# A grouped convolution whose stores bound it: whole images in 16 KB rows, and a second pipeline that lags by half a group

## The chip, the cores and the metric

One core of one Trainium2 chip. The metric is the device time of one execution in microseconds (us); a kernel is run several times and the median is quoted. The engines are called as in the profile: PE (TensorE's matmuls), PEld (its weight loads), DVE (VectorE), ACT (ScalarE), POOL (GpSimd), SP (SyncE). The 16 DMA engines are called transfer engines; where the text speaks of the ends, packets or chains of an engine, one of these is meant.

## The reference

A 3x3 convolution with padding 1 in 8 groups: 16 images of 64 channels and 64x64 points, 128 output channels, all fp32.

```python
batch, c_in, h, w, c_out, k, groups = 16, 64, 64, 64, 128, 3, 8
for g in range(groups):            # 8 input and 16 output channels per group
    for b in range(batch):
        for co in range(c_out_per_group):
            for ci in range(c_in_per_group):
                for kh in range(k):
                    for kw in range(k):
                        output[b, g*16 + co] += weight[g*16 + co, ci, kh, kw] * x_pad[b, g*8 + ci, kh:kh+h, kw:kw+w]
```

It reads 16.8 MB and writes 33.6 MB.

## The kernel before

Two pipelines share TensorE. Each handles two images at a time: a "group" is those two images, in four "sets" of 16 image rows, each set in four PSUM banks (512 points each). A set is nine taps, one per "slot", and three empty slots for the eviction: a period of 12 slots. The pipelines use different tiles of the array and are 6 slots apart.

```python
xn = [pool.tile([128, H, W], BF16, name=f"xn{i}") for i in range(4)]     # all inputs, cast to bf16 by the loads
xs = [pool.tile([128, H, W], BF16, name=f"xs{i}") for i in range(4)]
ob = [pool.tile([128, HALF], FP32, name=f"ob{i}") for i in range(NOB)]   # NOB = 16 half images
...
def finish(self, st):                    # evict a set; store after every second set
    i, s = st // 4, st % 4
    if s % 2 == 0:
        self.slots = [(nob[0] + im) % NOB for im in range(2)]
        ...
    for j in range(2):
        for im in range(2):
            ...
            eng, copy = ((ACT, nc.scalar.copy), (DVE, nc.vector.tensor_copy))[nev[0] % 2]
            eng.wait((stored[slot], 16 * uses[slot]) if uses[slot] else None, self.full[j, im])
            free[b] = eng.done(copy(ob[slot][:, o0 : o0 + 512], banks[b]))
    ...
    if s % 2 == 1:
        s0 = HALF * (s // 2)
        for im in range(2):
            ...
            nc.sync.dma_start(outf[img][:, s0 : s0 + HALF], ob[slot]).then_inc(stored[slot], 16)

pipes = (Pipe(0), Pipe(1))
PERIOD, LAG, NSETS = T + 3, (T + 3) // 2, 16          # 12, 6, 16
for slot in range(PERIOD * NSETS + LAG):
    ...                                               # the matmuls of the live pipelines, tile by tile
```

In a slot the weights of one tap are loaded once per tile and used for two matmuls:

```python
if j == 0:
    PE.wait(w_need[wt.name, 3 * kh + kw])
    pe.ldweights(w_ap, **pos)
```

Of the kernel before, what the change touches and what calls it, by code (L numbers as in the profile page):

```python
# [7 lines left out]
FP32 = mybir.dt.float32  # L8
# [4 lines left out]
@with_exitstack  # L13
def kernel(
    ctx: ExitStack,
    tc: tile.TileContext,
    x: bass.AP,
    weight: bass.AP,
    groups: int,
    out: bass.AP,  # L20
):
    nc = tc.nc

    B, C, H, W = x.shape
    CO, CIg, K, _ = weight.shape
    G = groups
    COg = CO // G
    HW = H * W
    T = K * K
    assert (B, C, CO, K, G, H, W) == (16, 64, 128, 3, 8, 64, 64)  # L30

    R = 8
    NCH = H // R
    HALF = HW // 2

    HALF = HW // 2
    NOB = 16

    pool = ctx.enter_context(tc.tile_pool(name="sb", bufs=1))
    psum = ctx.enter_context(tc.tile_pool(name="psum", bufs=1, space=bass.MemoryType.PSUM))  # L40

    xn = [pool.tile([128, H, W], BF16, name=f"xn{i}") for i in range(4)]
    xs = [pool.tile([128, H, W], BF16, name=f"xs{i}") for i in range(4)]
    ob = [pool.tile([128, HALF], FP32, name=f"ob{i}") for i in range(NOB)]
    w_sb = pool.tile([128, CIg * T], FP32, name="w_sb")
    mask = pool.tile([128, G], FP32, name="mask")
    ident = pool.tile([128, 128], BF16, name="ident")
    E = pool.tile([128, T, 160], BF16, name="E")
    wN = pool.tile([128, T, 128], BF16, name="wN")
    wS = pool.tile([128, T, 128], BF16, name="wS")  # L50
    banks = [psum.tile([128, 512], FP32, name=f"bank{i}") for i in range(8)]

    with tc.tile_critical():  # L53
        program(nc, x, weight, out, xn, xs, ob, w_sb, mask, ident, E, wN, wS, banks)
# [29 lines left out]
def program(nc, x, weight, out, xn, xs, ob, w_sb, mask, ident, E, wN, wS, banks):  # L84
    H = W = 64
    HW, HALF, T, G, CIg, COg, R = H * W, H * W // 2, 9, 8, 8, 16, 8
    NOB = len(ob)
    sems = []
# [6 lines left out]
    def sem(name):  # L95
        s = nc.alloc_semaphore(name)
        sems.append(s)
        return s
# [80 lines left out]
    outf = out.rearrange("b co h w -> b co (h w)")  # L179
    taps = [(1, 1)] + [(a, b) for a in range(3) for b in range(3) if (a, b) != (1, 1)]  # L180
    pe = nc.tensor
    stored = [sem(f"st{i}") for i in range(NOB)]
    uses = [0] * NOB
    nob = [0]
    nev = [0]

    class Pipe:
# [52 lines left out]

        def finish(self, st):
            i, s = st // 4, st % 4
            if s % 2 == 0:
                self.slots = [(nob[0] + im) % NOB for im in range(2)]
                self.wrote = [[], []]
                nob[0] += 2
            for j in range(2):
                for im in range(2):
                    slot, b = self.slots[im], self.banks[j][im]
                    o0 = 512 * (2 * (s % 2) + j)  # L250
                    eng, copy = ((ACT, nc.scalar.copy), (DVE, nc.vector.tensor_copy))[nev[0] % 2]
                    nev[0] += 1
                    eng.wait((stored[slot], 16 * uses[slot]) if uses[slot] else None, self.full[j, im])
                    free[b] = eng.done(copy(ob[slot][:, o0 : o0 + 512], banks[b]))  # L254
                    self.wrote[im].append(free[b])
                nev[0] += 1
            nev[0] += 1
            if s % 2 == 1:
                s0 = HALF * (s // 2)
                for im in range(2):  # L260
                    slot = self.slots[im]
                    img = 2 * i + 8 * self.k + im
                    SP.wait(*self.wrote[im])
                    nc.sync.dma_start(outf[img][:, s0 : s0 + HALF], ob[slot]).then_inc(stored[slot], 16)
                    uses[slot] += 1

    pipes = (Pipe(0), Pipe(1))
    PERIOD, LAG, NSETS = T + 3, (T + 3) // 2, 16
    for slot in range(PERIOD * NSETS + LAG):
        live = []  # L270
        for p, lag in zip(pipes, (0, LAG)):
# [10 lines left out]

    SP.wait(*((stored[s], 16 * uses[s]) for s in range(NOB)))
    POOL.wait(SP.done(nc.sync.nop()))
# [36 lines left out]
```

## Time and profile before

| | before |
|---|---|
| median time | 130.17 us (3 runs), 130.13 us (6 runs) |
| span of the profiled execution | 128.2 us |
| PE busy | 86.9 us, 68%; idle from 93.5 us on, the last eviction ends at 94.7 |
| stores / loads, share of the 16 transfer engines | 62.9% / 32.8% |
| store transfers | 32 of 1 MB, rows of 8 KB |

The profile is read by stretches: until 20 us loads alone, until 55 us loads and stores mixed, then stores alone, for the last 32 us with all compute engines idle. The columns of the list of DMA queues are packets, MB and share of the 16 transfer engines' time, as in this line:

```profile
q8 instruction: 13, 0.21, 0.6%
```

Thirteen packets of 16 KB each: TensorE's instructions, fetched while it runs (with about 1000 of them taken out, below, there are nine).

### The profile page before, as it was taken

The numbers are of one execution on the slowest core, as the hardware profiler recorded it, in microseconds if no ns is written. First come the engines' busy times: TensorE is split into PE (matmuls) and PEld (weight loads), VectorE is DVE, ScalarE is ACT, GpSimd is POOL, SyncE is SP. The second block draws the span as 40 slices with busy tenths as digits, with TensorE's granted clock in tenths as the row PEclk, the third lists the DMA queues.
The fourth block names the chain that finished last, engine by engine and source line by source line (L and its number), as shares of the span: only waits on it lengthen the run. The fifth ranks groups of instructions, "written<-read, shape, count | busy, mean of one in ns | idle before, by whom it ended". The sixth has DMA issues, their size and how long they took to land.

```text
span 128.2 us, 3808 instructions
## 1 busy us (share of the span) xinstructions
PE 86.9 (68%) x2322; PEld 41.2 (32%) x1170; DVE 45.8 (36%) x74; ACT 37.0 (29%) x68; POOL 7.2 (6%) x19
## 2 busy tenths in 40 slices
PE   0199999999999999999999999999910000000000
PEld 0153353544435355444553544544500000000000
DVE  1840465446444645446544564465440000000000
ACT  4030354345333543336333453354330000000000
POOL 5960000000000000000000000000000000000000
PEclk9999999999999999999999999999996555555555
DMA  2999999999999999999999999999999999999950
GB/s 24 162 202 215 224 212 220 215 289 284 281 289 281 284 271 297 297 401 424 419 424 424 396 435 406 435 414 429 417 424 429 424 432 422 429 427 432 427 243 10
DMA packets 6271, 42.21 MB, mean 329 GB/s; under 512 B 848, under 2 KB 848, under 8 KB 1424
## 3 DMA queue, kind: packets, MB, share of 16 engines
q1 hardware_dynamic: 4752, 33.59, 62.9%
q0 software_dynamic: 1504, 8.39, 32.8%
q8 instruction: 13, 0.21, 0.6%
q14 instruction: 2, 0.02, 0.0%
HBM read 16.81 MB, written 33.55 MB: 393 GB/s over the span
## 4 chain that ended last, share of the span: by engine, by line
PE 67%; DVE 4%; issue 2%; POOL 1%; POOLq 0%; DVEq 0%; SPq 0%
PE bank L227 65%; DVE E L149 2%; DVE ob L254 2%; PE bank L162 2%; POOL ident L128 0%; POOL mask L123 0%; POOL mask L133 0%; POOL xn L106 0%; POOLq L123 0%; POOLq L316 0%; DVEq L75 0%; SPq L53 0%
## 5 line engine op out<-in xcount | busy, mean ns | idle before, releaser
L227 PE MATMUL bank<-xs,wS 32*64 32x504 bf16 (+3 forms) x1152 | 71.6, 374 | 0.6 <-issue 0.4
L227 PE MATMUL bank<-xn,wN 32*64 32x504 bf16 (+3 forms) x1152 | 71.8, 380 | 0.2 <-DVE ob L254 0.2
L254 DVE COPY ob<-bank 128x512 f32<-128x512 f32 x64 | 41.3, 686 | 45.4 <-PE bank L227 45.4
L254 ACT COPY ob<-bank 128x512 f32<-128x512 f32 x64 | 34.5, 589 | 51.2 <-PE bank L227 51.1
L222 PEld LDWEIGHTS <-wS 32*64 32x64 bf16 x576 | 27.5, 104 | 20.8 <-issue 9.9
L222 PEld LDWEIGHTS <-wN 32*64 32x64 bf16 x576 | 19.1, 106 | 25.0 <-issue 20.9
L162 PE MATMUL bank<-ident,E 128*128 128x128 bf16 x18 | 2.1, 313 | 5.9 <-DVE E L149 5.9
L106 POOL DMA_DIRECT2D xs<-in_x_dram x7 | 3.8, 543 | 0.0
L162 PEld LDWEIGHTS bank<-ident,E 128*128 128x128 bf16 x18 | 1.8, 148 | 5.9 <-DVE E L149 5.9
L149 DVE TENSOR_TENSOR E<-w_sb,mask 128x288 bf16<-128x288 f32 x5 | 2.9, 642 | 1.7 <-DMA w_sb<-in_weight_dram 1.7
L106 POOL DMA_DIRECT2D xn<-in_x_dram x5 | 2.9, 583 | 1.0 <-SPq L53 1.0
L172 ACT CAST wS<-bank 128x512 bf16<-128x512 f32 (+1 forms) x3 | 1.2, 487 | 5.2 <-PE bank L162 5.2
L172 DVE CAST wN<-bank 128x512 bf16<-128x512 f32 (+1 forms) x3 | 1.5, 551 | 0.7 <-PE bank L162 0.7
L172 ACT ACT_TABLE_LOAD x1 | 1.3, 1283 | 1.0 <-SPq L53 1.0
L117 DVE MEMSET mask<- 128x8 f32 x1 | 0.1, 65 | 1.1 <-SPq L53 1.1
L128 POOL TENSOR_SCALAR_AFFINE_SELECT ident<-ident 128x128 bf16<-128x128 bf16 x1 | 0.3, 306 | 0.0
L123 POOL TENSOR_SCALAR_AFFINE_SELECT mask<-mask 128x8 f32<-128x8 f32 x1 | 0.2, 211 | 0.1
L133 POOL TENSOR_SCALAR_AFFINE_SELECT mask<-mask 128x8 f32<-128x8 f32 x1 | 0.2, 199 | 0.0
L302 POOL MEMSET const-float32-0.0<- 128x1 f32 x1 | 0.1, 99 | 0.3 <-issue 0.3
L118 DVE MEMSET ident<- 128x64 uint32 x1 | 0.1, 112 | 0.0
L302 POOL MEMSET const-bfloat16-1.0<- 128x1 bf16 x1 | 0.1, 102 | 0.0
L302 POOL MEMSET const-uint8-127<- 128x1 uint8 x1 | 0.1, 102 | 0.0
(1 smaller groups left out, 0.1 us busy)
## 6 DMA issues: line engine op xcount, KB each, us to landing
out_dram<-ob SPq DMA_DIRECT2D x32, 1024.0 KB, 28.0
xn<-in_x_dram POOLq DMA_DIRECT2D x3, 1024.0 KB, 29.6
xs<-in_x_dram POOLq DMA_DIRECT2D x2, 1024.0 KB, 29.6
xn<-in_x_dram POOLq DMA_DIRECT2D x2, 512.0 KB, 7.6
xs<-in_x_dram POOLq DMA_DIRECT2D x2, 512.0 KB, 9.4
xs<-in_x_dram POOLq DMA_DIRECT2D x1, 768.0 KB, 48.4
xs<-in_x_dram POOLq DMA_DIRECT2D x2, 128.0 KB, 9.5
w_sb<-in_weight_dram SPq DMA_DIRECT2D x1, 36.0 KB, 1.8
```

The costliest lines, as they stand in the source:

```text
L106: nc.gpsimd.dma_start(t.rearrange("p h w -> p (h w)")[p0:p1, h0 * W : h1 * W], xr[row0 + p0 : row0 + p1, h0 * W : h1 * W],).then_inc(s, 16)
L117: m1 = DVE.done(nc.vector.memset(mask, 1.0))
L123: m3 = POOL.done(nc.gpsimd.affine_select(out=mask, in_=mask, compare_op=ALU.is_ge, fill=0.0, base=0, channel_multiplier=1, pattern=[[-COg, ...
L128: m4 = POOL.done(nc.gpsimd.affine_select(out=ident, in_=ident, compare_op=ALU.not_equal, fill=1.0, base=0, channel_multiplier=1, pattern=[ ...
L133: m5 = POOL.done(nc.gpsimd.affine_select(out=mask, in_=mask, compare_op=ALU.is_ge, fill=0.0, base=COg - 1, channel_multiplier=-1, pattern= ...
L149: e = DVE.done(nc.vector.tensor_mul(E[:, :, 32 * r : 32 * r + 32].rearrange("p t (g c) -> p t g c", c=CIg), wv.unsqueeze(2).to_broadcast([ ...
L162: ins = nc.tensor.matmul(banks[b][:, 128 * t : 128 * t + 128], E[:, t0 + t, off : off + 128], ident, start=True, stop=True,)
L172: free[b] = eng.done(copy(dst, banks[b][:, 0 : 128 * n]))
L222: pe.ldweights(w_ap, **pos)
L227: ins = pe.add_instruction(mybir.InstMatmult(name=nc.get_next_instruction_name(), engine=mybir.EngineType.PE, start_tensor_calc=k == 0, st ...
L254: free[b] = eng.done(copy(ob[slot][:, o0 : o0 + 512], banks[b]))
L302: nc = _bacc.Bacc("TRN2", target_bir_lowering=False, num_devices=1)
```

## The change

The intent: longer store rows, so half as many packets; an image is stored when it is complete. Whole images need buffers of twice the size, so there are eight for sixteen. With eight, both pipelines in step would hold all four pairs at once; the second one is therefore moved back by half a group (24 slots), so that pairs come free one at a time.

```diff
-    NOB = 16
+    NOB = 8
-    ob = [pool.tile([128, HALF], FP32, name=f"ob{i}") for i in range(NOB)]
+    ob = [pool.tile([128, HW], FP32, name=f"ob{i}") for i in range(NOB)]
 ...
-            if s % 2 == 0:
+            if s == 0:
                 self.slots = [(nob[0] + im) % NOB for im in range(2)]
 ...
-                    o0 = 512 * (2 * (s % 2) + j)
+                    o0 = 512 * (2 * s + j)
 ...
-            if s % 2 == 1:
-                s0 = HALF * (s // 2)
+            if s == 3:
                 for im in range(2):
 ...
-                    nc.sync.dma_start(outf[img][:, s0 : s0 + HALF], ob[slot]).then_inc(stored[slot], 16)
+                    nc.sync.dma_start(outf[img], ob[slot]).then_inc(stored[slot], 16)
 ...
-    PERIOD, LAG, NSETS = T + 3, (T + 3) // 2, 16
+    PERIOD, LAG, NSETS = T + 3, (T + 3) // 2 + 2 * (T + 3), 16
```

More of the change, by code (lines that the diff above doesn't have):

```diff
@@ L34 @@
     HALF = HW // 2
-    HALF = HW // 2
-    NOB = 16
+    NOB = 8
     pool = ctx.enter_context(tc.tile_pool(name="sb", bufs=1))
```

## The prediction

> **What bounds the kernel now.** I read the two rows of slices first, because they show which resource is full and when. Of the page of the kernel before:
>
> ```profile
> PE   0199999999999999999999999999910000000000
> PEclk9999999999999999999999999999996555555555
> DMA  2999999999999999999999999999999999999950
> GB/s 24 162 202 215 224 212 220 215 289 284 281 289 281 284 271 297 297 401 424 419 424 424 396 435 406 435 414 429 417 424 429 424 432 422 429 427 432 427 243 10
> ```
>
> A slice is 128.2 / 40 = 3.2 us. TensorE works from slice 2 to slice 29 and then does nothing for ten slices, a quarter of the span. The DMA engines are at 9 in every slice from 1 to 37. So TensorE isn't the bound, although the chain of waits gives it 67% of the span; that chain follows instructions and stops at the last eviction, near 94.7 us. The remaining 33 us are stores that were issued and have still to land.
>
> The second view is the DMA queues, which give the work in the engines:
>
> ```profile
> q1 hardware_dynamic: 4752, 33.59, 62.9%
> q0 software_dynamic: 1504, 8.39, 32.8%
> HBM read 16.81 MB, written 33.55 MB: 393 GB/s over the span
> out_dram<-ob SPq DMA_DIRECT2D x32, 1024.0 KB, 28.0
> ```
>
> Stores take 0.629 x 128.2 = 80.6 us on all 16 engines, loads 0.328 x 128.2 = 42.0 us, together 122.7 of 128.2 us. Loads are counted by what they write, bf16; they read twice that, 16.8 MB of fp32. A store waits 28 us from issue to landing, 12 MB at the rate of the tail: a long queue stands behind the engines nearly all the time. A change that conserves bytes can therefore gain only by cheaper packets, and lose only by letting the DMA engines run dry.
>
> Third, the stretches of different mix (columns: PE, weight loads, DVE, ACT, POOL busy, clock, DMA share, GB/s):
>
> ```profile
> 9.60:19.20 9.60, 9.42 (x247) 3.95 (x123) 3.21 (x6) 2.82 (x6) 0.00 (x0) 1.00 1.06 217
> 21.00:54.00 33.00, 32.55 (x925) 15.42 (x461) 16.80 (x26) 14.06 (x26) 0.00 (x0) 1.00 1.02 274
> 56.00:80.00 24.00, 23.89 (x676) 11.22 (x337) 11.60 (x18) 9.66 (x18) 0.00 (x0) 1.00 1.01 420
> 99.00:122.00 23.00, 0.00 (x0) 0.00 (x0) 0.00 (x0) 0.00 (x0) 0.00 (x0) 0.50 1.01 427
> ```
>
> Loads alone write 217 GB/s, so they read 434. Mixed, the count is 274 to 297. Stores alone run at 420 to 427, and at 427 TensorE is off: no engine disturbs them there. Fourth, who waited for buffers:
>
> ```profile
> ACT ob L254 <- PE bank L227: 51.1, 32, 4.7
> DVE ob L254 <- PE bank L227: 45.4, 32, 5.5
> ```
>
> All waits of the two evicting engines are for TensorE, none for a store. The sixteen buffers are enough today.
>
> From the trace's packet records I took the durations of single packets. Loads: rows of 8 KB read take 324 ns (median), rows of 16 KB 624 ns. Stores of 8 KB: 322 ns beside loads, 309 ns alone, mean over all 4096 312.7 ns. Two equations for the loads, a + b = 324 and a + 2b = 624, give b = 300 ns for 8 KB and a = 24 ns for a packet of any size. With the same b a store has a = 22 ns in the mix and 9 ns alone.
>
> **What the Trainium skill says.** "DMA: Bandwidth & Descriptors", section "Where 436 GB/s comes from", puts the ceiling of the 16 ports at 435 GB/s. The trace agrees: 434 for loads and 427 for stores alone. The best that any row length can give the tail is 435 / 427, 1.9%. The same page, "Why small descriptors are slow (HBM only)", has a small fixed cost per packet, which it thinks worth attacking only at 256 B and less. The 9 to 24 ns above are 3 to 7% of an 8 KB packet, so here it is visible, but small. The same page, "Queues, rings and completion order", says that an engine takes turns between its queues by packet. The mix agrees: in equal 5 us stretches there are 76 to 96 store packets beside 79 to 92 load packets, one for one. And "TensorEngine Tiling (Array Packing)", "Key Properties", says that tiles work in parallel. The trace agrees: at the end, with the second pipeline alone, a slot of eight matmuls takes 0.43 us (weight loads at 90.45, 90.89, 91.32, 91.75), and with both pipelines in the array a slot of sixteen takes the same (11.55, 11.98, 12.41). Half of the array alone is half the throughput.
>
> **The change part by part.**
>
> (1) Stores in 16 KB rows. 4096 packets of 8 KB become 2048 of 16 KB; the semaphore packets halve (32 x 16 to 16 x 16). A packet alone becomes 9 + 600 = 609 ns instead of two of 309 = 618, in the mix 622 instead of 644. About a sixth of the stores (5.4 of 33.6 MB, below) goes in the mix, so the mean is near 611 ns. 2048 x 611 / 16 = 78.2 us, against 4096 x 312.7 / 16 = 80.05 us. Gain on the bound: **1.8 us**.
>
> (2) The lag grows from 6 slots to 30. The loop has 192 + 30 = 222 slots instead of 198. Evictions of one pipeline come every 5.15 us now ((93.4 - 13.5) / 31 = 2.58 us for half a period). A period of one pipeline alone isn't shorter: nine slots, then the wait for the banks; at 13.5 the first pair of copies (0.59 and 0.69 us, two in a row on each engine) delays the next set in just this way. So TensorE ends 24 x 0.43 = 10.4 us later, at about 105. This isn't on the path: DMA work then still stands in line.
>
> (3) The first store. It was issued at 20.0 us, after two sets; now it waits for four, 13.5 + 3 x 5.1 + 1.3 = 30 us. The gap is filled with loads: read bytes are 6.7 MB at 19 us, and at 0.43 MB per us 11.4 of 16.8 MB at 30 us. Then loads and stores take turns with packets of equal size, about 210 GB/s each (before: 16 KB against 8 KB, two thirds for the loads). The loads' last 5.4 MB take 26 us, until 56, and 5.4 MB are stored meanwhile. From there 28.2 MB at 430 GB/s take 65.5 us: 121.5. The same sum for the kernel before: from 54.5 us some 29.0 MB at 424, that is 122.9. The difference, 1.4 us, agrees roughly with (1). The real end is a few us after either, as some engines finish late (the last two slices: 243 and 10 GB/s) and the program closes after that; I take this as the same in both.
>
> (4) Does the queue run dry? A pair of images is 4.19 MB. Issues of the eight pairs, by 5.1 us per set and 13 us of lag: 30, 43, 51, 64, 71, 84, 92, 105 us. Each pair is through at 50, 63, 73, 82, 92, 102, 112, 121 us. Every pair is issued well before the one ahead of it is through; the least lead is some 7 us, at the last. Hence no idle time.
>
> (5) Does a buffer block? Eight buffers are four pairs; the third group of a pipeline reuses the pair of its first. First copies into reused pairs: 54, 67, 75 and 88 us; those stores are through at 50, 63, 63 + 10 = 73, and 82 us, plus some 2 us for landing. The first three are close, with 0 to 3 us to spare. Where one is missed, both evicting engines stand still (they serve both pipelines in order) and TensorE ends later by as much. With 7 us of lead at the last pair, a stall of 2 or 3 us costs nothing.
>
> Sum: -1.8 us from packets, about -0.2 us because more of the loads run alone (434 GB/s against 2L + S of about 416 in the mix: 4% on some 5 us), 0 from (2), (4) and (5): 130.2 - 2.0 = 128.2. As (1) assumes that the whole fixed cost of a packet is halved, I take a little back: **128.4 us**.
>
> **Rivals.**
> A: the row length does nothing, because at 427 GB/s the ports are nearly full. For it: 9 ns may be rounding of the drain and not a cost of the packet. Then the time is 129.5 to 130.2.
> B: the single-pipeline start stays slow. In the first 3.3 us slots last 0.80 us (weight loads at 8.35, 9.15, 9.95), and they become 0.43 us just when the second pipeline joins at 11.2 us. If it is the second pipeline that makes them fast, 30 slots run slow and everything on TensorE comes some 6 us later, the last pair at 111 us. Against it: the lone pipeline at the end is fast. Even then the queue has 1 us of work in hand at the closest points; if it runs dry the time is 129 to 132.
> C: the buffers block in a chain: one late store stalls both pipelines, the next pairs are issued late, and the DMA runs dry before the last. It needs over 7 us of stall in sum. Time 131 to 135.
> D: larger packets save more, and the mix profits as well (all with a = 24 ns: 4096 x 24 / 2 / 16 = 3.1 us). Time 127. Against it: the ceiling of 435.
>
> **Range and chances.** The mechanism is bounded on both sides: the ceiling lets the stores gain 1.9% of 80 us, 1.5 us, in the tail and a little more in the mix, and loss needs idle DMA engines, which the sums don't show. I expect 128.4, range 127.2 to 130.1. Faster by over 2% means under 127.6: 0.17. Slower by over 2%, over 132.8: 0.04. Within 2%: 0.79.
>
> **What would show it.** q1 with 2048 + 128 + 272 = 2448 packets and some 79 us of work; 16 stores of 2048 KB with about 17 us to landing; DMA at 9 in every slice up to the last two; loads' end (the jump to 420 GB/s) near 56 us; tail rate 430 to 434; TensorE until about 105 us with its slots at 0.43 us from the start of the lone stage; hardly any eviction that waits for a store. I'm wrong in step (1) if 16 KB packets take 618 ns or more, in (4) if a DMA slice falls under 9 before the end, in (5) if evictions wait for stores by more than 7 us.

## The result, and the profile after

129.92 us (129.54 to 130.22, 6 runs) against 130.13 us: ratio 0.9983, 95% interval 0.9964 to 1.0003. A repetition later gave 0.9998 (0.9979 to 1.0017). The change does next to nothing; 1.7 us of gain had been predicted.

The rows of slices of the changed kernel (3.2 us each), the counterpart of those that the prediction starts with:

```profile
PE   0198989999989797979998999999989790000000
DMA  2999999999999999999999999999999999999930
GB/s 29 158 185 209 226 214 214 220 214 186 288 329 332 306 324 339 296 385 419 434 429 424 434 419 429 413 419 434 429 419 429 439 419 424 444 429 424 424 153 10
```

PE works until 105.9 us and the last eviction ends at 107.0, the transfer engines are at 9 without a break, the loads run alone until slice 9 and are through at 57.7 us. The count in the mix is higher (288 to 339) because a turn of the stores now moves 16 KB, as much as a turn of the loads reads. In the last two slices the DMA row falls to 3 and 0 where it was 5 and 0: on average the transfer engines are done a little earlier. The queues and the stores (packets, MB, share; then KB each and us to landing), and who waited for buffers:

```profile
q1 hardware_dynamic: 2448, 33.59, 61.8%
q0 software_dynamic: 1504, 8.39, 33.1%
q8 instruction: 13, 0.21, 0.6%
out_dram<-ob SPq DMA_DIRECT2D x16, 2048.0 KB, 20.0
```

```profile
ACT ob L253 <- PE bank L226: 63.6, 33, 4.0
DVE ob L253 <- PE bank L226: 57.7, 33, 4.2
```

Nearly every sign that the prediction asked for is there: 2448 packets, 0.618 x 128.4 = 79.4 us of store work instead of 80.6, no eviction that waits for a store, no idle slice. Yet the span is 128.4 us, not shorter than 128.2. So the end was looked at by itself. These are the last us, 121 to 127, in 40 slices of 0.15 us, first of the kernel before, then of the changed one. One 8 KB packet per slice is 55 GB/s, one of 16 KB 109 GB/s.

```profile
DMA  6979999997969573723333231201010101000000
GB/s 273 546 328 437 437 382 492 382 437 328 382 273 382 218 328 164 328 109 164 164 164 164 109 164 55 109 0 55 0 55 0 55 0 55 0 0 0 0 0 0
```

```profile
DMA  7797559555755575255202000200020002000000
GB/s 328 328 765 328 219 218 546 218 218 218 328 218 218 218 328 218 109 218 218 109 0 109 0 0 0 109 0 0 0 109 0 0 0 109 0 0 0 0 0 0
```

A packet counts in the slice in which it starts. The rows thin out sooner in the changed kernel: from the 21st slice (124.0 us) on it starts 4 packets of 16 KB, the kernel before 18 of 8 KB. But it doesn't end earlier. In both the tail is a lone transfer engine that has packets left: before, the last four slices with 55; after, the last three with 109. All stores give every transfer engine the same bytes, and yet the 16 don't end together.

To put numbers to it I linked the packets of the trace into chains. The records don't name the transfer engine, but where stores run alone each packet begins 3 or 4 ns before the one ahead of it on its engine ends, which gives 16 chains. Who is linked with whom is a guess where several fit; the set of the 16 last ends isn't.

| profile | rows | lag | instruction fetches | mean of the four earliest ends | mean of all 16 | last but one | last |
|---|---|---|---|---|---|---|---|
| before | 8 KB | 6 | 13 | 122.5 | 123.8 | 125.1 | 126.4 |
| changed | 16 KB | 30 | 13 | 121.9 | 123.4 | 124.6 | 126.6 |

The four earliest gain 0.6 us, the mean 0.4, the last loses 0.2, and the last is what counts. Two questions follow: why is the gain 0.6 and not 1.8 us, and why did the last engine not share it?

### The profile page after: what moved, and what is told of

It reads as the page before. It is cut to its first block, busy times and chain, and to the rows that moved or that the text cites. A ratio compares the mean times of both kernels' runs of the same rounds, so it can differ in the third digit from the quotient of the medians. Undisturbed runs are those within 1.5% of the kernel's fastest.

```text
span 128.4 us, 3764 instructions
## 1 busy us (share of the span) xinstructions
PE 93.4 (73%) x2322; PEld 39.2 (31%) x1170; DVE 45.8 (36%) x74; ACT 37.0 (29%) x68; POOL 7.2 (6%) x19
## 3 DMA queue, kind: packets, MB, share of 16 engines
q1 hardware_dynamic: 2448, 33.59, 61.8%
## 4 chain that ended last, share of the span: by engine, by line
PE 67%; DVE 10%; issue 5%; POOL 1%; POOLq 0%; DVEq 0%; SPq 0%
PE bank L226 66%; DVE ob L253 8%; DVE E L148 2%; PE bank L161 2%; POOL ident L127 0%; POOL mask L122 0%; POOL mask L132 0%; POOL xn L105 0%; POOLq L122 0%; POOLq L314 0%; DVEq L74 0%; SPq L52 0%
## 5 line engine op out<-in xcount | busy, mean ns | idle before, releaser
L226 PE MATMUL bank<-xn,wN 32*64 32x504 bf16 (+3 forms) x1152 | 71.0, 375 | 2.7 <-DVE ob L253 1.3
L253 DVE COPY ob<-bank 128x512 f32<-128x512 f32 x64 | 41.3, 686 | 57.7 <-PE bank L226 57.7
L221 PEld LDWEIGHTS <-wS 32*64 32x64 bf16 x576 | 25.1, 104 | 27.4 <-issue 17.3
L221 PEld LDWEIGHTS <-wN 32*64 32x64 bf16 x576 | 19.6, 105 | 32.7 <-issue 28.7
```

The source lines that it names most:

```text
L226: ins = pe.add_instruction(mybir.InstMatmult(name=nc.get_next_instruction_name(), engine=mybir.EngineType.PE, start_tensor_calc=k == 0, st ...
```

## The experiments

They ran on several chips; each has runs of the kernel before beside it (11 or 12, medians 129.88 to 130.22 us), and ratios are to those.

**Theory 1**: a packet occupies its transfer engine for little more than its bytes; the 9 to 24 ns of the prediction are how long a packet is under way, and packets overlap. In the stretch of stores alone one begins every 306 ns at 8 KB (shown as 309) and every 607 ns at 16 KB (shown as 611), so a packet costs 5 ns: 2048 x 5 / 16 = 0.64 us for all. **Rival**: the rows do save 1.8 us, and the longer lag costs 1.6.

### Rows of 8 and of 4 KB in the changed kernel (a_rows8, a_rows4)

```diff
-                    nc.sync.dma_start(outf[img], ob[slot]).then_inc(stored[slot], 16)
-                    uses[slot] += 1
+                    for piece in range(n):              # n = 2 for 8 KB, 4 for 4 KB
+                        cols = slice(HW // n * piece, HW // n * (piece + 1))
+                        nc.sync.dma_start(outf[img][:, cols], ob[slot][:, cols]).then_inc(stored[slot], 16)
+                    uses[slot] += n
```

> The changed kernel, with each image stored by two transfers of 8 KB rows issued at the same moment; nothing else differs. Theory 1 (a packet occupies its engine only about 5 ns beyond its bytes: packets follow each other every 306 ns at 8 KB and every 607 ns at 16 KB): the engines finish 0.65 us later on average than in the changed kernel, time 130.2 to 130.8, ratio to the kernel before 1.000 to 1.005. Rival (the rows do save 1.8 us as predicted, and the longer lag costs 1.6 us): time about 131.7, ratio 1.012.

> The same with four transfers of 4 KB rows per image. Theory 1: 6144 packets more at 5 ns on 16 engines, 1.9 us over the changed kernel, 131.5 to 132.2; packets follow each other every 155 ns. The prediction's 9 ns: 3.5 us more, 133.4. Its 24 ns: 9 us more, 139.

a_rows8: 130.93 us, ratio 1.0073 (1.0055 to 1.0091). a_rows4: 132.81 us, ratio 1.0219 (1.0200 to 1.0238). The same stretch of stores alone, 99 to 121 us, of the changed kernel, of a_rows8 and of a_rows4 (the last number is GB/s):

```profile
99.00:121.00 22.00, 6.17 (x108) 1.81 (x48) 2.57 (x4) 2.15 (x4) 0.00 (x0) 0.78 1.01 430
```

```profile
99.00:121.00 22.00, 4.82 (x83) 1.17 (x36) 2.58 (x4) 2.15 (x4) 0.00 (x0) 0.75 1.01 427
```

```profile
99.00:121.00 22.00, 7.00 (x123) 2.24 (x56) 2.58 (x4) 2.15 (x4) 0.00 (x0) 0.77 1.03 414
```

From 8 to 16 KB the rate rises by 0.7%, from 4 to 8 KB by 3.1%. The four earliest transfer engines end at 121.9, 122.3 and 124.3 us. That is Theory 1 for the engines at 8 KB: 0.4 us, far from 1.8. At 4 KB its 5 ns were too few: the four earliest lose 2.4 us where 1.9 had been expected, 6 ns for each added packet, and the time of 132.81 us lies above the 131.5 to 132.2 of Theory 1 (and below the 133.4 of the prediction's 9 ns). The time of a_rows8 misses Theory 1 too: it is 0.9% over the changed kernel (1.2 us), between the two theories; in its profile the last engine ends at 127.6 us, 2.7 us after the last but one. So the row length and the last engine's delay are two things.

### The lag alone, and the rows alone (b_lag30, a_lag6)

```diff
 kernel before:   -LAG = (T + 3) // 2                  +LAG = (T + 3) // 2 + 2 * (T + 3)
 changed kernel:  -LAG = (T + 3) // 2 + 2 * (T + 3)    +LAG = (T + 3) // 2
```

> The kernel before with the longer lag alone (30 slots in place of 6), rows of 8 KB and sixteen half-image buffers kept. Theory 1 (the lag costs the bound nothing): ratio to the kernel before 0.997 to 1.004, TensorE ends near 106 us. Rival (the lag costs what the rows save): 131.7, ratio 1.012, with the transfers idle or slower somewhere between 20 and 60 us.

> The changed kernel with the old lag of 6 slots: 16 KB rows alone. Buffers should block: all four pairs are taken before the first store lands, both pipelines stand still together, the transfers run dry before the last pairs. Time 132 to 136, evicting engines wait for stores by more than 7 us. If the lag has nothing to do with the buffers: 129.9 and no such wait.

b_lag30: 130.66 us, 1.0054 (1.0035 to 1.0073): neither 1.000 nor 1.012. Its transfer engines end on average at 123.9 us and the earliest four at 122.6, the kernel before's times; the last at 127.0 instead of 126.4. a_lag6: 129.24 us, 0.9953 (0.9932 to 0.9973); I had expected it to lose. The evictions do wait for stores, as expected:

```profile
DVE ob L253 <- DMA out_dram<-ob: 9.0, 3, 4.3
ACT ob L253 <- DMA out_dram<-ob: 8.8, 1, 8.8
```

But the stop of some 9 us comes at 56 us, when the transfer engines have whole images standing in line; they don't run dry, and the last eviction, off the path, ends at 102.9 us, with less lag to run off at the end. The step that failed in my expectation was to count the stop and not what stood in the queue meanwhile. The earliest engines end at 121.9 us as in the changed kernel, the last at 125.7. Again a difference that sits in the last engine alone.

### One engine relieved (a_k15)

```diff
+                    if self.k == 1 and i == 3 and im == 1:      # the very last image
+                        lo, hi = slice(0, HALF), slice(HALF, HW)
+                        for rows, cols in ((slice(0, 128), lo), (slice(0, 120), hi), (slice(120, 128), hi)):
+                            nc.sync.dma_start(outf[img][rows, cols], ob[slot][rows, cols]).then_inc(stored[slot], 16)
+                        uses[slot] += 3
```

> So far the span ends with one engine of the 16 that finishes 1.2 to 2.7 us after the next one, in each of the profiles. Here the second half of the last image of the changed kernel is stored as 120 partitions (spread over 15 engines) and 8 partitions (over 8), so one engine is given 2.4 us less and eight of the others 0.3 us more; the bytes are the same. If the time is set by the one late engine and it is the one relieved: 1 to 2 us less than the changed kernel, ratio to the kernel before 0.985 to 0.992. If it is one of the others: 0.998 to 1.002. If not one late engine but the sum of the work sets the time: 0.998, and the last landings spread as before.

130.75 us, 1.0040 (1.0019 to 1.0061). One chain now ended at 119.6 us, ahead of all others, so one engine was relieved as meant (the queue of stores has 23 semaphore packets of 4 bytes more than in the changed kernel, 15 + 8); the last ended at 127.5. The late one thus isn't the one that this split relieves. A split by hand, without knowing who is late, made it worse.

### Fewer instruction fetches (a_few, a_nops, a_few_split)

In the stretch of stores alone the chains show what an instruction fetch does: it holds one transfer engine for 0.88 to 0.97 us, and the data packet behind it takes some 0.4 us longer (1005 ns, say, for 611): 1.3 us of one engine. Thirteen of them over 16 engines are 1.1 us on average, but they may fall unevenly. Hence a new theory: the last engine is the one that fetches fell on most. a_few takes out about 1000 of TensorE's instructions (wrong results):

```diff
                 if j == 0:
                     PE.wait(w_need[wt.name, 3 * kh + kw])
-                    pe.ldweights(w_ap, **pos)
+                    if k == 0:
+                        pe.ldweights(w_ap, **pos)
```

> The changed kernel without the weight loads of eight of the nine taps (wrong results on purpose; the same matmuls, evictions and transfers): about 1000 fewer TensorE instructions, so some 4 fewer of the 13 instruction fetches of 16 KB, each of which holds one transfer engine for some 1.2 us. If fetches make an engine late: the engines finish 0.3 us earlier on average and the last up to 1.2 us earlier, ratio to the kernel before 0.990 to 0.996. If the late engine has another cause: 0.996 to 0.999.

128.40 us, 0.9858 (0.9839 to 0.9876): 1.25% under the changed kernel, more than any other edit gained, and more than the 0.990 to 0.996 that the theory allowed. The list of queues shows the fetches:

```profile
q8 instruction: 9, 0.15, 0.4%
```

The earliest four engines end at 121.7 us, just as in the changed kernel; the last at 125.0 instead of 126.6. So nothing was gained for an undisturbed engine. But fewer weights are read and fewer instructions run as well. The first of these was to be told apart. The first attempt put instructions that do nothing in the place of the loads:

> The kernel with fewer weight loads ran 1.25% faster than the changed kernel. Here each weight load that was taken out there is replaced by an instruction of TensorE that does nothing (results wrong on purpose as there), so the number of instructions is again that of the changed kernel and the weights are still not read. If the instruction fetches cost the time: 13 fetches again, ratio to the kernel before 0.996 to 1.000. If reading the weights did: 9 fetches' worth of gain stays, 0.984 to 0.989.

128.40 us, 0.9883 (0.9862 to 0.9905), and 9 fetches, not 13: the instructions hadn't reached the chip. It tells nothing of the cause, and serves as a repetition of a_few. The second attempt left the loads out and cut the matmuls of four taps into two halves of the image rows, which reads the same data with about 1000 more instructions:

```diff
+                mid = (lo + hi) // 2 if k in (1, 3, 5, 7) else hi
+                for r0, r1 in ((lo, mid), (mid, hi)):
+                    ...                                  # the same matmul, on image rows r0 to r1
```

> The instructions that do nothing had been dropped on the way to the chip (9 fetches in that profile too), so it told nothing of fetch against weight reading. Here the weight loads of eight taps are left out again (wrong results on purpose), and the matmuls of four taps are cut into two halves each, which reads the same data in about 1000 more instructions: 13 fetches, weights not read. If the fetches cost the time: ratio to the kernel before 0.996 to 1.002, the changed kernel's. If reading the weights did: 0.985 to 0.990 as without the weight loads.

129.87 us, 0.9982 (0.9962 to 1.0002): the changed kernel's time, with its fetches and without its weight loads.

```profile
q8 instruction: 13, 0.21, 0.6%
```

The last engine ends at 126.6 us again, the earliest four at 121.8. So about 1000 TensorE instructions fewer gain 1.0 to 1.2% (1.3 to 1.6 us), and reading the weights isn't the reason. But in these edits the fetches go with the instructions, so the times don't tell these two apart, and four fetches are only 4 x 1.3 / 16 = 0.3 us on average. The Trainium skill, "Runtime: NRT & Kernel Launch", section "Instruction fetch mechanics", has the blocks of 16 KB (256 instructions) and calls the cost of crossing one "mostly hidden". The 13 packets agree with the block: 16 sets x 2 pipelines x 9 taps x 12 instructions, and 36 that prepare the weights, are 3492, and 3492 / 256 = 13.6. From the transfers a fetch isn't hidden: it holds its engine as told above.

**What makes the last engine late.** The packet records tell fetches and instructions apart. From the end of the loads on, each profile has store packets that take a little longer than the usual 611 ns: 629 to 747 ns (at 8 KB, 327 to 418 in place of 309). Those behind a fetch, at about 1005 ns, are not meant.

- They are the packets of one transfer engine. In the changed kernel there are 65 after 60 us. Nearly always the next one begins 3 to 14 ns before the one ahead of it ends; three times exactly one usual packet lies between. An instruction fetch has no room there. The same holds in a_few (62) and a_few_split (69).
- This engine is the one that ends last. Followed on from the last lengthened packet, its chain ends as the last of all in 14 of the 17 profiles followed so, in nine of them, a_few and a_few_split included, without any fork. (In b_lag30, a_rows8 and a_k15 the links lead elsewhere.)
- They come only while stores run alone and TensorE works. In the kernel before, the changed kernel, a_lag6, a_few and a_few_split at most one of the 269 to 549 store packets up to 1 us before the end of the loads is such a packet, and none of the 424 to 1574 after the last matmul; in the stop of a_lag6, from 60.2 to 65.2 us, none of 128.
- What they take beyond the usual goes with the number of TensorE's instructions, matmuls or weight loads: 2.5 to 2.7 ns for each that is recorded after the end of the loads, in all profiles of the table below. (a_lag6_shift64, whose queue ran dry, has 3.2.)
- This sum, put on the mean end of the four earliest engines, gives the last end within 0.5 us:

| profile | TensorE instructions after the loads | added to one engine's packets, us | four earliest + added | last end | ratio |
|---|---|---|---|---|---|
| before | 1542 | 4.10 | 126.6 | 126.4 | 1 |
| b_lag30 | 1741 | 4.48 | 127.1 | 127.0 | 1.0054 |
| a_rows8 | 1977 | 4.95 | 127.3 | 127.6 | 1.0073 |
| changed | 1717 | 4.39 | 126.3 | 126.6 | 0.9983 |
| a_same | 1790 | 4.63 | 126.4 | 126.9 | 0.9998 |
| a_lag6 | 1588 | 4.22 | 126.1 | 125.7 | 0.9953 |
| a_lag18 | 1553 | 4.12 | 126.0 | 125.7 | 0.9946 |
| a_few | 1196 | 3.07 | 124.8 | 125.0 | 0.9858 |
| a_few_split | 1779 | 4.62 | 126.4 | 126.6 | 0.9982 |

So the new theory fails: from 60 us to the end of TensorE's work the last engine met no fetch. Between a_few and a_few_split its packets are lengthened by 1.55 us more, about the 1.6 us in the last end and the 1.3 to 1.6 us in the time. It also explains a_rows8: there the loads are through at 50.0 us already, and more of TensorE's work falls in the time of stores alone. What happens in the 2.6 ns isn't shown; no packet of its own stands in the records. Nor is it shown that an execution which isn't recorded has them: every timed run here was recorded with its span and clock.

### More fetches (a_split)

> The changed kernel with all its weight loads and the matmuls of four taps cut into halves (right results): 17 fetches in place of 13. If the fetches cost the time, by the 1.2 to 1.6 us that four fewer gained: ratio 1.008 to 1.012. If not: 0.997 to 1.001, as long as TensorE ends before 112 us.

136.74 us (135.97 to 139.33), 1.0529; two of the six runs, at 138.21 and 139.33 us, were slow, and the four fast ones alone are 4.8% over the kernel before. That is far over both, so it tells nothing of the fetches. Cutting the matmuls with all weight loads kept slows TensorE until it ends near 119 us, past the 112 us that I had named as the limit, and the transfer engines run dry:

```profile
DMA  2999999999999999999997999499709999999990
GB/s 24 166 212 215 226 212 220 212 217 195 342 315 312 327 334 295 417 410 439 410 439 337 449 400 391 205 391 434 278 5 381 444 400 425 420 395 405 439 420 34
```

The slices with 205, 278 and 5 GB/s are stores that weren't there yet. It shows what the prediction's rivals B and C would have looked like; nothing of the kind is in the changed kernel. (After the last dry spell all engines start together, and 12 of the 16 end within 0.2 us of each other, at 131.1 to 131.3 us: the unevenness is collected on the way, not at the end.)

### Is it the lag, or where the fetches fall? (a_same, a_few_lag6, a_lag18, and five with the fetches moved)

The lag of 30 had cost 0.5% with 8 KB rows. With 16 KB rows and 18 slots:

> The changed kernel with a lag of 18 slots, halfway. With 6 slots the ratio to the kernel before was 0.9953, with 30 it was 0.9983. If the lag itself makes the engines finish later: between the two, 0.995 to 0.998. If it was the stop of the pipelines at 6 slots that helped: 0.998 or more, since at 18 slots there is less or no stop.

129.53 us, 0.9946 (0.9927 to 0.9965). The next call repeated the changed kernel and took the lag back with few fetches:

> The changed kernel once more, unedited, as the row of reference of this call, and to see how far the ends of the 16 engines differ from one profile of the same program to the next: ratio to the kernel before 0.996 to 1.000, one engine again 1 to 2.5 us after the next one.

> The kernel with fewer weight loads and the old lag of 6 slots (wrong results on purpose). If the lag costs time because of where the fetches fall: the same as with 30 slots, 0.984 to 0.988. If the lag costs it by itself: 0.3% less, 0.981 to 0.984.

a_same: 129.99 us, 0.9998 (0.9979 to 1.0017). a_few_lag6: 128.27 us, 0.9866 (0.9846 to 0.9887), no faster than 0.9858 and 0.9883 with the lag of 30. With nine fetches the lag costs nothing that these runs resolve. I took that to speak for the place of the fetches, so they were moved, by cutting the matmuls of four taps in the first set (64 instructions more) or the first two (128 more), results right:

```diff
+                mid = (lo + hi) // 2 if st == 0 and k in (1, 3, 5, 7) else hi      # st <= 1 for 128
```

> The changed kernel (lag 30) with 64 more instructions on TensorE in the first set (the matmuls of four taps cut into halves, right results), so each of the 13 fetches comes a quarter of a fetch earlier. If the lag itself costs 0.4%: ratio to the kernel before 0.997 to 1.001. If the place of the fetches decides: anything from 0.993 to 1.003, and the last engine's distance from the undisturbed ones changes with it.

> The same with 128 more instructions, in the first two sets: half a fetch earlier. Lag: 0.997 to 1.001. Place of the fetches: anything from 0.993 to 1.003.

> The lag of 6 with 16 KB rows and the same 64 instructions more. Lag: 0.993 to 0.997, as without them. Place of the fetches: anything from 0.993 to 1.003.

> The lag of 6 with 16 KB rows and the same 128 instructions more. Lag: 0.993 to 0.997. Place of the fetches: anything from 0.993 to 1.003.

> 16 KB rows with a lag of 18 slots, unedited, with more rounds. The lag itself costs time: 0.993 to 0.997. Chance of that one call: 0.997 to 1.000.

> The same with 128 more instructions on TensorE in the first two sets. The lag itself: 0.993 to 0.997. The place of the fetches: anything from 0.993 to 1.003.

All ratios with 16 KB rows, right results and all weight loads:

| lag | as it is | 64 more | 128 more |
|---|---|---|---|
| 6 | 0.9953 | 1.0019 | 0.9956 |
| 18 | 0.9946, 0.9965 | - | 0.9988 |
| 30 | 0.9983, 0.9998 | 0.9991 | 0.9984 |

(The added instructions also bring a 14th fetch into four of these five profiles, so they aren't a pure move.) In the row of 30 nothing moves: neither the place nor the 14th fetch shows there. In the row of 6, 64 instructions cost as much as the whole lag (the intervals, 0.9932 to 0.9973 and 0.9997 to 1.0041, don't meet); but there the stop of the evictions was 10.2 us and seven transfer engines then stood still for 0.4 to 1.0 us at 103 us, so it is also the first sign of a dry queue. In the row of 18 one run is at 0.9988, with an interval of 0.9969 to 1.0007. By what was on record before the last call, this isn't settled.

The count of instructions settles most of it, though it was read from the traces afterwards and has no run of its own. The two runs with a lag of 18 had 1553 and 1536 TensorE instructions left when the loads ended, those with 6 (without the dry queue) 1588 and 1628: 0.9946 to 0.9965. The four with 30 had 1717 to 1790, and the one with 18 and 128 more had 1813: 0.9983 to 0.9998. So neither the lag as such nor the place of the fetches is needed: how much of TensorE's work is left for the time when stores run alone fits all of these runs. (The two runs with a lag of 18 also had a stop: DVE waited 5.3 and 5.5 us for stores, and in the one with 128 more not at all. My expectation for a_lag18 had counted on less or none.)

## Why the prediction was wrong, point by point

**Step (1) failed, by a size.** "A packet alone becomes 9 + 600 = 609 ns instead of two of 309 = 618, in the mix 622 instead of 644." The durations came true (611 and 624 ns). But a packet's duration isn't the time that it occupies its engine: the next one begins before it ends, by 3 to 4 ns among stores and by 19 ns among loads. The term "1.8 us" should have been the cadence, 2 x 306 - 607 = 5 ns per pair of packets, 0.64 us in all; the ends of the four earliest engines measured 0.6. The sum of durations did fall, 80.04 to 78.94 us, and that is just what misleads. Rival A ("the row length does nothing") was nearer, and the check by rates was in the prediction's own hands: loads at 434 GB/s are 8 KB every 302 ns on each engine, where a packet shows 324.

**Step (2) failed in its zero.** "This isn't on the path", and before it "A change that conserves bytes can therefore gain only by cheaper packets, and lose only by letting the DMA engines run dry." TensorE ended as predicted (105.9 us, 105 said) and no engine ran dry, yet the lag alone cost 0.54% (0.7 us) in b_lag30: it leaves TensorE more instructions for the time when stores run alone (1741 for 1542), and these lengthen the packets of the one engine that ends last. In the changed kernel this takes back 0.3 us (4.39 for 4.10), in its repetition 0.5. The prediction had shown a sign that TensorE's work costs the transfers something, 420 GB/s with it and 427 without, and made nothing of it.

**The closing remark of step (3) failed too.** "The real end is a few us after either, as some engines finish late ...; I take this as the same in both." The spread from the earliest four to the last was 3.9 us before and 4.7 us after. It was as large as the whole question, and it took the 0.6 us. Of the 0.8 us, 0.3 are the added lengthening; the rest isn't explained. The two profiles' last ends differ by +0.2 us, the medians by -0.2; both mean that nothing was left.

The measured 129.92 us lies inside the stated range, near its upper end, but not by the prediction's mechanism: that is luck.

**The 0.2 us for more loads alone** wasn't seen: the loads' packets took 41.8 us (on 16 engines) before and 42.2 after. As these are durations, it is no proof.

**Steps (4) and (5) held**: every transfer engine was busy to its end, no eviction waited for a store.

**Rival B** is refuted: with the second pipeline absent until slot 30, the first nine slots (72 matmuls) took 4.4 us, which is 0.49 us each, not 0.80. **Rivals C and D** didn't occur; the stall of C was seen in miniature with a lag of 6.

**The median wait of a store** was 20.0 us, not 17; why isn't shown.

Shown: the row length is worth 0.6 us to an undisturbed transfer engine; the last of 16 engines sets the end; its packets are lengthened by 2.5 to 2.7 ns for each TensorE instruction while stores run alone; about 1000 instructions fewer take 1.3 to 1.6 us off the time, with the weight reads excluded as a cause. Argued only: that the fetches spread the other fifteen engines. Open: what lengthens the packets, and some 0.5 us of the last end in the changed kernel.

The best right kernels are those with 16 KB rows and a lag of 18 or 6 slots: 0.3 to 0.5% under the kernel before in three runs as they are, from 0.4% under to 0.2% over it with instructions added, and within 2% like the rest.

## What to carry to other kernels

When the transfer engines are the bound, take a packet's cost from the cadence of packets or the rate in a pure stretch, not from the packets' durations; and look at how the 16 engines end, as the last of them is the time. Follow that last one back: here it alone was slowed, packet by packet, in step with TensorE's instructions. Between rows of 8 and of 16 KB there is 0.7% of rate to gain; about 1000 TensorE instructions fewer gained more, and instructions that ran before the loads were through lengthened nothing. A stop of an engine off the path is free as long as enough stands in the queue.

## What the Trainium skill lacked or had wrong

- "Runtime: NRT & Kernel Launch", "Instruction fetch mechanics": it looks at the cost of a 16 KB block to the engine that fetches. That a fetch holds one transfer engine for about 1.3 us isn't said.
- "DMA: Bandwidth & Descriptors", "Why small descriptors are slow (HBM only)": it would pack only descriptors of 256 B and less. For stores to HBM from 128 partitions the rate still rose from 414 (4 KB) to 427 (8 KB) and 430 GB/s (16 KB).
- The same page: that a packet's duration in the trace is longer than the time that it occupies the engine, as packets overlap (309 ns shown, one every 306 ns; loads overlap by 19 ns), isn't said.
- No page says that TensorE's instructions lengthen the store packets of one transfer engine (2.5 to 2.7 ns each, 2.7 to 5.0 us in all), so that of 16 engines with equal bytes the last ends up to 5.3 us after the four earliest. The DMA page lists two engines as usually slower, with a guess at another cause; the records here don't name the engine.
